# A two-layer decoder trunk on one core: split weights two tiles further ahead, gate weights in the activation ring, rotary tables after the first stage

## The chip, the core and the metric

The kernel runs on one core of a Trainium2 chip. The metric is device time in microseconds from start to end of one execution, as the median of several runs. TensorE (PE) multiplies matrices, VectorE (DVE) and ScalarE (ACT) work element by element, GpSimd (POOL) does a few steps, SyncE (SP) issues nearly all DMAs.

## The reference

Two layers, 256 positions, width 2048, all in 32-bit floats. In each layer one normalised input goes through one projection (`w_in`) into five parts: queries, keys and values of eight heads of differential attention, and the two branches of a gated linear recurrence (RG-LRU). Both groups are concatenated, go through `w_out` and are added to x. Then comes an MLP with a causal convolution of three taps.

```python
h = rmsnorm(x, attn_norm[l])
q, k, v, xb, gb = jnp.split(h @ w_in[l], splits, axis=-1)
q, k = apply_rope(q, cos, sin), apply_rope(k, cos, sin)
attn_out = diff_attention(q, k, v, lam, subln[l], lam_init)
lru_out = rglru_branch(xb, gb, ...)     # conv of 4 taps, two gates, scan, norm
x = x + concat(attn_out, lru_out) @ w_out[l]
h = rmsnorm(x, mlp_norm[l])
x = x + conv_glu_mlp(h, w_up[l], ffn_conv_w[l], ffn_conv_b[l], w_down[l])
```

`cos` and `sin` come from the positions. The gates are eight blocks of 128 x 128 weights each, for two gates. `decay` below is a softplus of `lru_lambda` by a series, and `lambda` the scalar of the differential attention.

## The kernel before, in words

**Weights.** All weights stream through the core once, 1 MB at a time: `raw` tiles of 128 x 2048 floats, 200 units per layer, in the order of the list `stream`. There are three raw buffers. Each `raw` is cut into two tiles of 128 x 1024. ACT rounds a tile to the matmul's format (`hi`, line 174), DVE subtracts to get the remainder (`lo`, line 181). Activations are split in the same way (`xh`: high and low side by side, lines 296 and 300). A product is then two matmuls: `hi` times both activation parts (512 columns) and `lo` times the high part (256 columns). Such a pair for one 128 x 128 piece of weights is called a block; a tile is eight blocks.

**Order.** The order of every engine is the order in which the Python code emits instructions; there is no scheduler. `run` (line 246) emits 16 blocks at a time, two tiles: first one side of all 16, then the other; the next run starts with the side on which this one ended, so every second run starts with its low parts. While it takes blocks, `next_blocks` emits the `hi` tile that lies `HI_LEAD` ahead at a tile's start, and in its middle the `lo` tile that lies `LO_LEAD` ahead and the DMA that a finished raw tile makes room for. All other work is deferred: `defer(n, fn)` emits `fn` once TensorE's instructions have come n blocks further. A list of such steps (`steps`) is the schedule of each piece: tables of cosine and sine (`setup_tables`), `setup_decay`, `setup_lambda`, the LRU (`lru_front`, `lru_back`), a head (`attention`). Since an engine takes its instructions in order, a step that waits holds up what was emitted behind it.

**Stages of a layer.** First the eight column pairs of the LRU (`rb`, 32 blocks each) and the value projection (`pv`, in quarters of 16 blocks); then the heads (`qk`), the output projection (`po`) and the MLP (`pu`, `pd`), each with all 24 tiles of a half's hidden values in the ring `actp`, which has 24 buffers. Layer 0 begins with `first_stage`: inputs arrive feature by feature, and for each pair of features k, k+1 TensorE does two LRU column pairs (`recurrent`) and half of the values (`values`). `prepare` makes high and low parts there in halves of 512 columns (lines 888 and 889), and TensorE's instructions are emitted `LEAD` features behind. Gate weights lie in a fixed tile `gw_sb` of 1 MB, loaded by `later_inputs` in layer 0 and at the start of layer 1. After two column pairs, `lru_back` does their gates (`gp`, line 535), four ACT functions for each, square root, scan and `gate`, then a square (line 588) and a sum for the norm. For a head: `turns`, `rope`, `scores`, softmax, `difference` (line 695), `turn` (transposes on TensorE, line 703), `values`, a norm and `back`.

Lines after the change are some ten to twenty higher than before from line 536 on.

## Time and profile before

| | us |
|---|---|
| median of three runs | 2334.37 |
| lowest, highest | 2333.59, 2338.35 |
| the profiled execution | 2339.55 |
| its span, first to last instruction | 2337.7 |
| TensorE busy in the span | 2302.3 (98%) |
| VectorE busy | 1655.5 (71%) |
| ScalarE busy | 1290.1 (55%) |
| mean granted TensorE clock | 0.995 |

The busy time of TensorE is that of its matmul records, whose ends are modelled; neighbouring matmuls overlap in it. In a row of a timeline stand start, length, engine, line, operation, tiles written and read, shape and count; in brackets the idle time of the engine ahead of it and what ended that. A row of waits names who waited, for whom, the total in us, how often and the longest. A row of windows gives a stretch, its length, the busy time of each engine with its instructions, the granted clock (1.00 is full speed), the share of the DMA engines and GB/s.

### The profile page before, as it was taken

Reading aid. Unit: us, or ns where it says so; the run is one execution under the profiler, and the core shown is the slowest. Engines: PE = TensorE matmul, PEld = TensorE weight load, DVE = VectorE, ACT = ScalarE, POOL = GpSimd, SP = SyncE. Lnnn points to the kernel's source line nnn. Section 1 sums busy time; section 2 is a strip of 40 time slices with the busy share of each in tenths; the row PEclk is TensorE's granted clock in tenths of the full one; section 3 lists DMA queues with packets and bytes.
Section 4 is the critical chain, followed back from the end, with each engine's and each line's share of the span. In section 5 each row is a group of like instructions: output and inputs, shape, how many; then the busy total and the mean of one; then the engine's idle time right before and its main releaser. Section 6 shows DMA issues by size and latency. Waiting matters only on the chain.

```text
span 2337.7 us, 33496 instructions
## 1 busy us (share of the span) xinstructions
PE 2302.3 (98%) x13196; PEld 2020.9 (86%) x13196; DVE 1655.5 (71%) x2321; ACT 1290.1 (55%) x1930; POOL 38.5 (2%) x148
## 2 busy tenths in 40 slices
PE   8999999999999999999999999999999999999998
PEld 6887888888888888888888888888888888888887
DVE  7677877777754677775567797777776557777654
ACT  6775645555543455554457666455555335555543
POOL 0000000000000000000000000000000000000000
PEclk9999999999999999999999999999999999999999
DMA  7344445455555455555455444555454545455543
GB/s 266 145 162 155 155 165 196 181 196 195 186 180 199 181 197 191 188 182 200 177 198 180 180 152 160 183 193 196 181 194 185 198 181 198 180 197 193 187 180 126
DMA packets 63229, 428.93 MB, mean 183 GB/s; under 512 B 7136, under 2 KB 7904, under 8 KB 12640
## 3 DMA queue, kind: packets, MB, share of 16 engines
q1 hardware_dynamic: 62352, 425.74, 49.7%
q8 instruction: 103, 1.69, 0.3%
q10 hardware_dynamic: 720, 1.07, 0.1%
q14 instruction: 54, 0.44, 0.1%
HBM read 424.68 MB, written 2.10 MB: 183 GB/s over the span
## 4 chain that ended last, share of the span: by engine, by line
PE 70%; issue 12%; DVE 11%; ACT 6%; DMA 1%; SPq 0%; POOL 0%; DVEq 0%; POOLq 0%; ACTq 0%
PE pu L264 34%; PE pd L264 17%; PE qk L264 5%; PE po L264 4%; DVE lo L181 4%; PE rb L264 3%; PE po_None L264 2%; ACT hi L174 2%; DVE cc L779 1%; DMA raw<-in_w 1%; DVE us L765 1%; PE pv L845 1%; PE pv L846 1%; PE pv L844 1%; DVE us L276 0%
## 5 line engine op out<-in xcount | busy, mean ns | idle before, releaser
L181 DVE TENSOR_TENSOR lo<-raw,hi 128x1024 fp32r<-128x1024 f32 x784 | 938.5, 1219 | 194.1 <-ACT hi L174 110.4
L174 ACT ACTIVATE hi<-raw 128x1024 fp32r<-128x1024 f32 x784 | 806.9, 1052 | 343.1 <-PE pd L264 183.2
L264 PE MATMUL pu<-xhm,hi 128*128 128x512 f32 x3008 | 700.9, 390 | 0.6 <-DVE x L959 0.4
L264 PEld LDWEIGHTS pu<-xhm,hi 128*128 128x128 f32 x3008 | 558.4, 188 | 113.4 <-issue 0.8
L264 PEld LDWEIGHTS pu<-xhm,lo 128*128 128x128 f32 x3008 | 373.7, 192 | 9.5 <-DVE lo L181 1.1
L264 PE MATMUL pu<-xhm,lo 128*128 128x256 f32 x3008 | 377.0, 283 | 1.6 <-DVE lo L181 0.9
L264 PE MATMUL pd<-h,hi 128*128 128x512 f32 x1512 | 352.0, 390 | 0.0
L264 PEld LDWEIGHTS pd<-h,hi 128*128 128x128 f32 x1512 | 280.7, 188 | 56.3
L779 DVE SCALAR_TENSOR_TENSOR cc<-us,cst_sb,cc 128x256 f32<-128x256 f32 x384 | 177.8, 483 | 42.0 <-ACT cc L772 35.2
L264 PEld LDWEIGHTS pd<-h,lo 128*128 128x128 f32 x1512 | 187.9, 192 | 3.7
L264 PE MATMUL pd<-h,lo 128*128 128x256 f32 x1512 | 189.2, 283 | 0.0
L772 ACT ACTIVATE cc<-us,cst_sb 128x256 f32<-128x256 f32 x192 | 105.6, 595 | 98.4 <-DVE us L765 98.4
L276 DVE TENSOR_TENSOR us<-pu,us 128x512 f32<-128x512 f32 x92 | 63.3, 688 | 122.9 <-ACT us L273 122.9
L963 DVE TENSOR_TENSOR x<-pd,x 128x512 f32<-128x512 f32 x56 | 38.7, 691 | 128.6 <-PE pd L264 127.7
L273 ACT ACTIVATE us<-pu 128x512 f32<-128x512 f32 x92 | 55.2, 600 | 114.8 <-PE pu L264 114.8
L785 ACT ACTIVATE cc<-cc 128x256 f32<-128x256 f32 x96 | 40.2, 419 | 66.8 <-DVE cc L779 66.3
L791 ACT ACTIVATE h<-cc 128x256 fp32r<-128x256 f32 x96 | 40.1, 417 | 53.0 <-DVE cc L788 50.0
L765 DVE TENSOR_TENSOR us<-us,row_m 128x512 f32<-128x512 f32 x96 | 65.4, 682 | 3.2
L264 PE MATMUL qk<-xhn,hi 128*128 128x512 f32 x256 | 62.0, 394 | 0.0
L264 PE MATMUL qk<-xhs,hi 128*128 128x512 f32 x256 | 61.9, 393 | 0.0
L264 PE MATMUL rb<-xhn,hi 128*128 128x512 f32 x256 | 61.0, 393 | 0.0
L264 PEld LDWEIGHTS qk<-xhn,hi 128*128 128x128 f32 x256 | 46.9, 188 | 11.6 <-issue 2.3
(257 smaller groups left out, 2123.7 us busy)
## 6 DMA issues: line engine op xcount, KB each, us to landing
raw<-in_w SPq DMA_DIRECT2D x392, 1024.0 KB, 4.8
raw<-in_w SPq DMA_DIRECT2D x12, 512.0 KB, 8.2
raw<-in_w SPq DMA_DIRECT2D x8, 256.0 KB, 6.4
gw_sb<-in_gw SPq DMA_DIRECT2D x2, 1024.0 KB, 10.0
x<-in_x SPq DMA_DIRECT2D x7, 256.0 KB, 7.8
out<-x ACTq DMA_DIRECT2D x4, 256.0 KB, 2.4
out<-x SPq DMA_DIRECT2D x4, 256.0 KB, 2.4
cst_sb<-in_cst SPq DMA_DIRECT2D x1, 425.0 KB, 10.6
```

The costliest lines, as they stand in the source:

```text
L174: act.activation(out=hi_t[v], in_=raw_part(v), func=AF.Copy)
L181: dve.tensor_tensor(out=lo_t[v], in0=raw_part(v), in1=hi_t[v].bitcast(F32), op=ALU.subtract)
L264: pe.matmul(out=dst, lhsT=taken[i][side], rhs=o, start=first and side == sides[0], stop=last and side == sides[1], skip_group_check=True,)
L273: act.activation(out=dst, in_=pb[:, :, SEQ:], func=AF.Copy)
L276: dve.tensor_tensor(out=dst, in0=pb[:, :, 0:SEQ], in1=dst, op=ALU.add)
L765: dve.tensor_tensor(out=dst, in0=dst if source is None else source, in1=row, op=ALU.mult)
L772: act.activation(out=cc[:, s], in_=us[:, s, 1:SEQ + 1], func=AF.Identity, scale=ccol(l, C_FCW + 3 * tiles[s]), bias=ccol(l, C_FCB + tiles[s]),
L779: dve.scalar_tensor_tensor(out=cc[:, s], in0=us[:, s, j + 1:j + 1 + SEQ], scalar=ccol(l, C_FCW + 3 * tiles[s] + j), in1=cc[:, s], op0=ALU. ...
L785: act.activation(out=cc[:, 0], in_=cc[:, 0], func=AF.Gelu_apprx_tanh)
L791: act.activation(out=t[:, 0], in_=cc[:, 0], func=AF.Copy)
L844: pe.matmul(out=pv[:, tb], lhsT=th_, rhs=wh, start=(k == 0), stop=False)
L963: dve.tensor_tensor(out=x_sb[i], in0=pb[:, :, s * SEQ:(s + 1) * SEQ], in1=x_sb[i], op=ALU.add)
```

## The change

The edits:

- High and low parts: `HI_LEAD` from 3 to 5, `LO_LEAD` from 2 to 4, two more buffers for each. The feature lead of the first stage goes from 2 to 4.
- `pos_sb` moves to the ring `t1`; the fixed tile `gw_sb` is gone. `load_gates` loads the gate weights in four DMAs into four buffers of the ring `actp`, in each layer, and the last gates give them back.
- In layer 0 the first value quarter of the second half (unit 20) comes between the column pairs 2 and 3 instead of behind all of them.
- The tables start 150 blocks into the kernel instead of 48, and their steps lie further apart; decay starts at 60 instead of 40, lambda at 100 instead of 150, the late DMAs at 24 instead of 16.
- LRU: square three blocks later, its sum four.
- Heads 0 to 6: `scores` to `turned` three blocks later, `values` to `low` four. Head 7 keeps its steps, but for `values` to `normed`, which come one block later.
- First stage: from the third unit on, parts are made as in the rest of the kernel, 1024 columns at a time; the norm's sum starts 24 blocks after the last pair instead of 13.
- The end of the first stage makes parts up to five tiles ahead of the first tile behind it.

```diff
-LEAD = 2
+LEAD = 4
-HI_LEAD = 3
-LO_LEAD = 2
+HI_LEAD = 5
+LO_LEAD = 4
-HI_BUFS = 5
-LO_BUFS = 4
+HI_BUFS = 7
+LO_BUFS = 6
...
-    pos_sb = t1.tile([P, SEQ], I32, tag="ti1", name="pos_sb", bufs=1)
-    gw_sb = const.tile([P, 2 * LT, P], F32, name="gw_sb")
+    pos_sb = t1.tile([P, SEQ], I32, tag="t1", name="pos_sb")
...
-            order = [*range(4, 16)]
+            order = [4, 5, 20, *range(6, 16), 21, 22, 23]
...
-            (0, angle), (6, coarse), (14, less_coarse), (18, turns), (32, reduced), (40, lambda: mirrored(1)),
-            (46, lambda: folded(1)), (50, lambda: mirrored(-1)), (56, lambda: folded(-1)), (60, sines), (70, signed),
+            (0, angle), (8, coarse), (24, less_coarse), (30, turns), (50, reduced), (64, lambda: mirrored(1)),
+            (76, lambda: folded(1)), (84, lambda: mirrored(-1)), (96, lambda: folded(-1)), (104, sines), (120, signed),
...
-                        out=tl["gp"][i][:, g * SEQ:(g + 1) * SEQ], lhsT=gw_sb[:, g * LT + j0 + i], rhs=xc[:, i],
+                        out=tl["gp"][i][:, g * SEQ:(g + 1) * SEQ], lhsT=gate_w[g * LT + j0 + i], rhs=xc[:, i],
...
+            if j0 == LT - 2:
+                gate_w.clear()
...
-            (n + 37, square), (n + 42, summed),
+            (n + 40, square), (n + 46, summed),
...
-            n = 83 if h == HEADS - 1 else 94
+            if h == HEADS - 1:
+                a, b, c = 19, 51, 83
+            else:
+                a, b, c = 22, 54, 98
...
-                (5, turns), (8, rope), (19, scores), (22, maxima), (29, exps), (35, weights), (38, second),
-                (41, difference), (51, turn), (54, turned), (62, values), (65, squares), (69, mean), (74, normed),
-                (n, back), (n + 3, high), (n + 7, low),
+                (5, turns), (8, rope), (a, scores), (a + 3, maxima), (a + 10, exps), (a + 16, weights),
+                (a + 19, second), (a + 22, difference), (b, turn), (b + 3, turned), (b + 12, values), (b + 15, squares),
+                (b + 19, mean), (b + 24, normed), (c, back), (c + 3, high), (c + 7, low),
...
-        state["hi"] = state["lo"] = tiles
+        state["hi"] = state["lo"] = 4 * FINE // 2
...
+            if u >= FINE:
+                if k % 2:
+                    hi_to(2 * u + 1)
+                    lo_to(2 * u + 1)
+                return
...
-                    n.finish(13)
+                    n.finish(24)
...
-                if i >= KD - 4:
-                    t = tiles + (i - KD + 4) // 2
-                    hi_to(t + 1)
-                    lo_to(t)
+                if i >= KD - 6:
+                    hi_to(tiles + (i - KD + 6) + 1)
+                    lo_to(tiles + (i - KD + 6))
...
+    def load_gates(l):
+        for i in range(4):
+            t = actp.tile([P, 4, P], F32, tag="a", name=f"gw{l}_{i}")
+            sync.dma_start(out=t, in_=gw[l][:, 4 * i:4 * i + 4])
+            for b in range(4):
+                gate_w[4 * i + b] = t[:, b]
...
-                defer(16, later_inputs)
-                defer(40, setup_decay)
-                defer(48, setup_tables)
-                defer(150, setup_lambda)
+                defer(24, later_inputs)
+                defer(60, setup_decay)
+                defer(100, setup_lambda)
+                defer(150, setup_tables)
...
+                if l == 0 and j == 2:
+                    pv = value_banks(l, 1)
+                    value_quarter(l, 1, 0, pv)
+            if l:
+                pv = value_banks(l, 1)
-            for quarter in range(4):
+            for quarter in range(1 - l, 4):
```

How the instructions move is seen at three places. The first is DVE's queue around the last unit of the first stage before the change: `rest` and `turns` are the tables, `xhs` the activations' low parts, `lo` the weights'.

```order
L318 TENSOR_TENSOR acc_n_first<-acc_n_first,xq_n_first_513 128x512
L397 SCALAR_TENSOR_TENSOR rest<-turns,ang 128x2x256
L399 SCALAR_TENSOR_TENSOR rest<-turns,rest 128x2x256 x2
L399 SCALAR_TENSOR_TENSOR rest<-many,rest 128x2x256
L409 TENSOR_TENSOR rest<-rest,turns 128x2x256
L300 SCALAR_TENSOR_TENSOR xhs_553<-x_107,gain_sb,xhs_553 128x256
L889 TENSOR_TENSOR lo_557<-raw_386,hi_556 128x512
L889 TENSOR_TENSOR lo_561<-raw_386,hi_560 128x512
L300 SCALAR_TENSOR_TENSOR xhs_564<-x_107,gain_sb,xhs_564 128x256
L889 TENSOR_TENSOR lo_557<-raw_386,hi_556 128x512
L889 TENSOR_TENSOR lo_561<-raw_386,hi_560 128x512
```

After the change the same queue, one unit earlier, holds only that unit's own steps between the end of the decay's series (`q`) and its close.

```order
L447 SCALAR_TENSOR_TENSOR q<-q,z_415 128x16 x8
L300 SCALAR_TENSOR_TENSOR xhs_485<-x_106,gain_sb,xhs_485 128x256
L300 SCALAR_TENSOR_TENSOR xhs_488<-x_106,gain_sb,xhs_488 128x256
L181 TENSOR_TENSOR lo_495<-raw_341,hi_491 128x1024
L181 TENSOR_TENSOR lo_497<-raw_341,hi_493 128x1024
L318 TENSOR_TENSOR acc_n_first<-acc_n_first,xq_n_first_499 128x512
L452 SCALAR_TENSOR_TENSOR q<-q,z 128x16
```

The tables have left this stage, and four low parts of 512 columns have become two of 1024.

The second place is SP's queue, before the change, where the late inputs are loaded; `raw_323` is the seventh weight unit (raw6).

```order
L160 DMA raw_266<-in_w 128x1024 x2
L950 DMA gw_sb<-in_gw 128x2048
L951 DMA kc_sb<-in_kc 128x130
L952 DMA pos_sb<-in_pos 128x256
L953 DMA cst_sb<-in_cst 128x850
L954 DMA lam_sb<-in_lamv 128x512
L160 DMA raw_323<-in_w 128x1024 x2
```

After the change (`raw_281` is the seventh unit here, `raw_341` the eighth, raw7):

```order
L160 DMA raw_281<-in_w 128x1024 x2
L963 DMA gw_0_300<-in_gw 128x512
L963 DMA gw_1_302<-in_gw 128x512
L963 DMA gw_2_304<-in_gw 128x512
L963 DMA gw_3_306<-in_gw 128x512
L969 DMA kc_sb<-in_kc 128x130
L970 DMA pos_sb<-in_pos 128x256
L971 DMA cst_sb<-in_cst 128x850
L972 DMA lam_sb<-in_lamv 128x512
L160 DMA raw_341<-in_w 128x1024 x2
```

The late inputs stand one weight unit later, and are eight issues instead of five.

The third place is ACT's queue in layer 0's LRU stage, at the back steps of the column pairs 2 and 3 (`sq_2` is their root, `gl` a gelu, the last row the square), before:

```order
L567 ACTIVATE sq_2_1044<-th_2_664 128x2x256
L510 ACTIVATE xc_4_910<-xg_4_911,cst_sb 128x256
L511 ACT_TABLE_LOAD
L511 ACTIVATE gl_4_907<-xg_4_911 128x256
L174 ACTIVATE hi_1083<-raw_939 128x1024
L570 ACTIVATE th_2_664<-u_2_1011,mones 128x512
L174 ACTIVATE hi_1096<-raw_986 128x1024
L588 ACTIVATE gl_2_663<-bx_2_665 128x512
```

and after:

```order
L569 ACTIVATE sq_2_1068<-th_2_644 128x2x256
L510 ACTIVATE xc_4_933<-xg_4_934,cst_sb 128x256
L511 ACT_TABLE_LOAD
L511 ACTIVATE gl_4_930<-xg_4_934 128x256
L412 ACT_TABLE_LOAD
L412 ACTIVATE trig_sb<-rest 128x512
L174 ACTIVATE hi_1109<-raw_961 128x1024
L572 ACTIVATE th_2_644<-u_2_1035,mones 128x512
L174 ACTIVATE hi_1122<-raw_1009 128x1024
L174 ACTIVATE hi_1165<-raw_1009 128x1024
L590 ACTIVATE gl_2_643<-bx_2_645 128x512
```

The sine of the tables (`trig_sb`) and a load of its function stand between the gelu and the next high part, and one more high part stands ahead of the square.

More of the change, by code (lines that the diff above doesn't have):

```diff
@@ L140, in trunk_kernel @@
                 order += [16 + quarter, 8 + 2 * quarter, 9 + 2 * quarter]
-        order += [*range(20, U_IN)]
+            order += [20, 21, 22, 23]
+        order += [*range(24, U_IN)]
         for half, i in PROJECTED:
@@ L916, in first_stage @@
                 prepare(k + 1)
-                raw_t.pop(k // 2)
+                raw_t.pop(k // 2, None)
                 square_pair(k // 2, n)
@@ L941, in first_stage @@
                     lo_t.pop(i + g)
-                if i >= KD - 4:
-                    t = tiles + (i - KD + 4) // 2
-                    hi_to(t + 1)
-                    lo_to(t)
+                if i >= KD - 6:
+                    hi_to(tiles + (i - KD + 6) + 1)
+                    lo_to(tiles + (i - KD + 6))
         state["at"] = tiles * SB
         defer(4, lambda: values_out(0, 0, pv))
+    gate_w = {}
+    def load_gates(l):
[4 more added lines that the diff above has]
+                gate_w[4 * i + b] = t[:, b]
     def later_inputs():
-        sync.dma_start(out=gw_sb, in_=gw[0])
+        load_gates(0)
         sync.dma_start(out=kc_sb[:, P:], in_=kc[:, P:])
@@ L1046, in trunk_kernel @@
             if l:
-                sync.dma_start(out=gw_sb, in_=gw[l])
+                load_gates(l)
             else:
-                defer(16, later_inputs)
-                defer(40, setup_decay)
-                defer(48, setup_tables)
-                defer(150, setup_lambda)
+                defer(24, later_inputs)
+                defer(60, setup_decay)
+                defer(100, setup_lambda)
+                defer(150, setup_tables)
                 first_stage()
@@ L1061, in trunk_kernel @@
                     value_quarter(l, 0, j - 3, pv)
-            pv = value_banks(l, 1)
-            for quarter in range(4):
+                if l == 0 and j == 2:
[4 more added lines that the diff above has]
+            for quarter in range(1 - l, 4):
                 value_quarter(l, 1, quarter, pv)
```

## The prediction

> **What bounds the kernel now.** I read the page first, then the stages by windows, then TensorE's waits by stage, and last the engines' timelines around the longest waits.
>
> ```profile
> span 2337.7 us, 33496 instructions
> PE 2302.3 (98%) x13196; PEld 2020.9 (86%) x13196; DVE 1655.5 (71%) x2321; ACT 1290.1 (55%) x1930; POOL 38.5 (2%) x148
> ```
>
> TensorE (PE) is busy for 98% of the span. So the change can win only what TensorE now waits, and what it loses to a lower clock. The windows show where (after the times: PE, PEld, DVE, ACT, POOL busy, granted clock, DMA share, GB/s):
>
> ```profile
> 5.00:56.00 51.00, 43.41 (x208) 34.74 (x207) 40.69 (x83) 30.55 (x59) 5.49 (x9) 1.00 0.78 278
> 56.00:63.00 7.00, 6.53 (x18) 5.37 (x19) 4.46 (x9) 3.72 (x5) 0.82 (x3) 0.51 0.52 164
> 97.00:104.00 7.00, 6.18 (x19) 5.26 (x20) 5.54 (x7) 2.53 (x4) 0.10 (x1) 0.51 0.59 215
> 104.00:128.00 24.00, 21.68 (x125) 19.06 (x124) 16.37 (x23) 19.64 (x29) 0.10 (x1) 1.00 0.30 113
> 128.00:131.40 3.40, 3.40 (x11) 2.81 (x11) 3.36 (x5) 0.93 (x1) 0.00 (x0) 0.53 0.85 308
> 160.00:291.00 131.00, 126.14 (x740) 106.36 (x739) 105.12 (x180) 82.84 (x188) 5.75 (x7) 1.00 0.42 157
> 400.00:1180.00 780.00, 780.00 (x4528) 692.31 (x4528) 536.42 (x714) 404.20 (x537) 4.43 (x43) 1.00 0.52 190
> ```
>
> From 400 to 1180 us (the MLP) TensorE never stops: more lookahead is worth nothing there. Layer 0 up to 291 us holds the waits and three spells at about half clock. A spell loses half of what TensorE worked in it: 6.53 x 0.49 = 3.2 us, 6.18 x 0.49 = 3.0 and 3.40 x 0.47 = 1.6, together 7.8.
>
> The waits of TensorE by stage (total, times, longest), in the order 0 to 60, 60 to 160, 160 to 300, 360 to 400 and 1180 to 1540 us:
>
> ```profile
> PE rb L904 <- DVE lo L889: 3.4, 3, 1.7
> PE rb L899 <- DVE xhs L300: 2.0, 2, 1.6
> PE ss_n_first L327 <- DVE acc_n_first L322: 1.5, 1, 1.5
> ...
> PE rb L264 <- DVE lo L181: 5.0, 3, 2.3
> PE pv L845 <- DVE lo L181: 0.5, 1, 0.5
> ...
> PE at L703 <- DVE pr L695: 3.9, 5, 1.3
> PE qk L264 <- DVE lo L181: 0.6, 1, 0.6
> ...
> PE pu L264 <- DVE lo L181: 0.9, 1, 0.9
> ...
> PE rb L264 <- DVE lo L181: 2.7, 3, 1.8
> ```
>
> These are 6.9 us in the first stage, 5.5 in layer 0's LRU stage, 4.5 in its attention, 0.9 at the start of its MLP and 2.7 in layer 1's LRU stage: 20.5 us. With the clock 28.3 us, which is all there is to win. Nearly every wait is for a low part or for another step of VectorE (DVE).
>
> **Part by part.** *First stage.* Two pieces of the DVE's and ACT's timelines show why low parts come late (lo of two halves; counters and angle of the tables; the decay's series):
>
> ```profile
> 31.51 1.29 DVE L889 TENSOR_TENSOR lo<-raw,hi 128x512 fp32r<-128x512 f32 x2
> 34.20 1.94 DVE L447 SCALAR_TENSOR_TENSOR q<-q,z 128x16 f32<-128x16 f32 x8
> 36.85 0.88 DVE L383 SCALAR_TENSOR_TENSOR ang<-many,ang 128x256 f32<-128x256 f32 x2
> 38.04 1.69 DVE L889 TENSOR_TENSOR lo<-raw,hi 128x512 fp32r<-128x512 f32 x2
> ...
> 47.13 1.42 DVE L399 SCALAR_TENSOR_TENSOR rest<-turns,rest 128x512 f32<-128x512 f32 x2
> 50.58 0.69 DVE L409 TENSOR_TENSOR rest<-rest,turns 128x512 f32<-128x512 f32 x1 [1.30 <-POOL turns L405]
> ...
> 37.88 1.30 POOL L390 TENSOR_SCALAR turns<-ang 128x256 f32<-128x256 f32 x2 [2.60 <-DVE ang L383]
> 45.87 1.28 ACT L412 ACT_TABLE_LOAD   x1
> 56.12 0.63 ACT L412 ACTIVATE trig_sb<-rest 128x512 f32<-128x512 f32 x1 [8.97 <-DVE rest L409]
> ```
>
> DVE is busy 40.69 of 51 us. The tables' rows here (0.88, 1.42, 0.69 and 1.30 of waiting) stand directly ahead of low parts that TensorE waits for. With them gone, halves merged into 1024-wide steps, and two more buffers, the late ones (all but about 1.4 us, early waits for data) should disappear: 6.9 - 1.4 = 5.5 us. The decay stays, but TensorE now has up to three units in hand instead of two. What is late next is data: 8 MB of weights, x, and the constants. Constants move behind raw6 and ahead of raw7; SP issues in order, so raw7 waits for its turn behind eight issues. A unit lasts TensorE 16 blocks. I cost that at nothing, because raw7 is needed two units later; uncovered it is the second rival below. Without the waits at 52 to 56 us I expect the spell at 56 us gone too: 3.2 us.
>
> *LRU stage of layer 0.* A block (one 512-wide high and one 256-wide low matmul) costs 11.11 / 32 = 0.347 us by this piece of the chain:
>
> ```profile
> 342.88 11.11 PE po L264 x64
> ```
>
> A run makes the low parts of the run behind it, and in a run that starts on low parts they are due 11 to 13 blocks after being issued: 3.8 to 4.6 us. Two more tiles add one run, 16 blocks or 5.5 us. The three waits (5.0 us, longest 2.3) are shorter than that, so as waits for lo they go, with the 0.5: 5.5 us, and with them the two spells, 3.0 + 1.6. But another wait stands right behind. ACT and DVE run a loop from one pair's gate matmuls to the taps of the next pair (rows of PE, then of ACT, then of DVE):
>
> ```profile
> 74.50 1.89 PE L535 MATMUL gp<-xc,gw_sb 128*128 128x256 f32 x8
> 97.82 2.08 PE L264 MATMUL rb<-xhs,lo 128*128 128x256 f32 x8 [1.24 <-DVE lo L181]
> 127.22 1.60 PE L264 MATMUL rb<-xhs,lo 128*128 128x256 f32 x8 [2.32 <-DVE lo L181]
> ...
> 104.14 0.47 ACT L545 ACTIVATE th<-gp,hb_sb 128x256 f32<-128x256 f32 x1 [4.62 <-PE gp L535]
> 122.52 0.63 ACT L588 ACTIVATE gl<-bx 128x512 f32<-128x512 f32 x1 [3.46 <-DVE bx L584]
> 123.06 1.04 ACT L174 ACTIVATE hi<-raw 128x1024 fp32r<-128x1024 f32 x1
> ...
> 127.08 1.52 DVE L515 SCALAR_TENSOR_TENSOR xc<-xg,cst_sb,xc 128x256 f32<-128x256 f32 x3
> ```
>
> From 104.14 to 127.08 + 1.52 it takes 24.5 us. TensorE needs 64 blocks (22.2 us) and eight gate matmuls (1.89): 24.1 us. So gate matmuls would wait about 0.4 us per pair in place of lo. The square behind `gate`, three blocks later, falls behind one more high part, and ACT's wait of 3.46 shrinks by its 1.04: loop 23.5. The value quarter between pairs gives the first loop 16 blocks (5.5 us) more, enough for the table's DVE rows there. The sine, however, falls between two gelus of the second loop: a load, the sine and a load back, 1.28 + 0.63 + 1.28 = 3.2 us, so 26.7 against 24.1. I charge 2.6 us, and 1.6 for a spell like the one at 128 us, which followed the wait of 2.32. Net gain: 10.1 - 4.2 = 5.9 us; the ends are 10.1 (the sine is hidden by parts made ahead) and 0 (every loop waits as now).
>
> POOL's table steps move along. In the rows above two low parts took 1.69 us while POOL worked, 1.29 without: 0.4 per pair of steps, about 1.6 us over the tables, which the first loop's 5.5 us hide. [...]
>
> *Attention.* Scores to `difference` and `turn` move three blocks back, 1.04 us. Of five waits for `pr` (3.9, longest 1.3) about 1.0 would remain, and the 0.6 for lo goes. But DVE has 105.12 of 131 us to do already, and one value quarter fewer now lies between LRU and heads, so the last pair's force and scans fall into head 0. I take 3.2 of 4.5; the ends are 0 and 4.5.
>
> *The rest.* The wait of 0.9 for lo at the MLP's start goes. Layer 1's three (2.7) go as lo, less 0.5 for one wait for the loop: 2.2. Gate weights in the activation ring wait for the last `pd` to release four hidden tiles; on SP only raw205 queues behind them, which is not due for four tiles, so nothing. Layer 1's first gates come 25 blocks after its second pair of columns. MLP: nothing.
>
> **Sum.** 5.5 + 3.2 + 5.9 + 3.2 + 0.9 + 2.2 = 20.9 us. The profiled execution took 2339.55 us (its span is 2337.7), 5.2 above the median of 2334.37; 20.9 off gives 2318.7 for a profiled one and 2313.5 for the median.
>
> **Rivals.**
>
> (a) *Slower: the loop bounds layer 0.* If ACT and DVE, not lookahead, set the pace, the tables go onto the loop's path: 3.2 us on ACT, on DVE 5.1 (0.88, four `rest` steps at 0.71, two folds at 0.69), 1.6 for POOL: 9.9. Each of three gate waits then passes the 2.32 us that had a spell behind it and costs a long spell's 3.2, 9.6 for the 4.6 now. That is +14.9, less 8.7 won in the first stage: +6.2, 2341. It decides once waits for gp in layer 0 add up to more than 14 us. For it speaks ACT's 19.64 of 24 us; against it, that ACT's rows above show 4.62 and 3.46 of idling. 0.05.
>
> (b) *The first stage is bound by data.* DMA is at 0.78 over it. If raw7 comes late behind the constants, the 8.7 us there stay: 2322. 0.12.
>
> (c) *The spells don't hang on these waits.* No single wait ahead of them lasted over 2.32 us, so something else may lower the clock at these places. Then the spells stay as they are, and 3.2 + 3.0 (those at 56 and 97 us; the third is charged already) come off the sum: 2320. Against it: the spells of 97 and 128 us begin within 1 us of the waits at 97.82 and 127.22, and in the 780 us without a wait the clock is 1.00. 0.08. [...]
>
> (d) *Nothing takes the place of the waits:* all 28.3 us go, 2306. 0.20.
>
> (e) *The lookahead is not reached,* because three raw buffers stay: high parts five tiles ahead wait for DMA. Then of the sum only the first stage's 5.5 us are left: 2329. Against it: from 400 to 1180 us DMA is at 0.52. 0.06.
>
> The forecast itself: 0.49.
>
> The range takes in the ends of the terms: 2304 (all of 28.3, and 2 for what a wait's row leaves out) to 2326 (first stage alone, 8.7). About 0.2%, 4.7 us, is what a measurement of this kernel can tell from no change. Case (e) lies so near that bound that I count 0.04 of it as same; (a) is slower, the rest faster: 0.91, 0.04, 0.05.
>
> **What would show it.** Right: no waits for lo L181 at rb in either layer; the clock at 1.00 around 56 us; waits for gp on xc of 2 to 3 us in one loop, where the sine stands on ACT; the MLP unchanged. Wrong: waits for raw or for xhs before 56 us (b); half-clock spells without waits (c); waits for xc at every pair (a); idle ACT ahead of hi with DMA as releaser (e).

## The result and the profile after

| | median of its runs, us | lowest to highest | ratio to before, 95% interval |
|---|---|---|---|
| before (4 runs) | 2335.91 | 2333.59 to 2338.35 | |
| after (4 runs) | 2319.94 | 2317.67 to 2321.37 | 0.9931 [0.9913, 0.9948] |
| after, again (5 runs, before 2335.65) | 2317.61 | 2316.85 to 2321.92 | 0.9929 [0.9916, 0.9941] |

The change makes the kernel 16 to 18 us faster, within the range, where 20.9 was forecast. The profiled execution of after took 2321.12 us.

```profile
span 2319.3 us, 33304 instructions
PE 2292.8 (99%) x13196; PEld 2016.9 (87%) x13196; DVE 1654.7 (71%) x2309; ACT 1290.5 (56%) x1919; POOL 40.9 (2%) x148
```

TensorE does the same 13196 matmuls, and the span is 18.4 us shorter than the 2337.7 of before. The starts of the first matmul of each stage in PE's timeline give the stages; "again" is a second profiled execution of after, and "best" is the last experiment:

| stage, us | before | after | again | best | after less before | forecast |
|---|---|---|---|---|---|---|
| first stage | 59.08 | 53.94 | 50.54 | 46.68 | -5.1 | -8.7 |
| rest of the LRU, layer 0 | 106.46 | 100.90 | 100.92 | 97.97 | -5.6 | -5.9 |
| heads, layer 0 | 112.11 | 107.84 | 107.82 | 103.71 | -4.3 | -3.2 |
| output projection | 93.99 | 94.13 | 94.15 | 94.14 | +0.1 | 0 |
| MLP | 803.27 | 803.26 | 803.26 | 803.25 | 0.0 | -0.9 |
| LRU, layer 1 | 143.89 | 140.47 | 140.47 | 140.45 | -3.4 | -2.2 |
| heads, layer 1 | 105.16 | 103.45 | 103.45 | 103.43 | -1.7 | 0 |
| output projection and MLP, layer 1 | 908.60 | 909.98 | 909.99 | 910.00 | +1.4 | 0 |

The rows of the heads and of what follows them have to be read together. Eight small matmuls of the heads run in the output projection after the change, in both layers (heads 632 matmuls where before had 640, output projection 552 where it had 544), because the last steps of the heads come four blocks later. With the heads' steps put back (an experiment below) layer 1's heads take 104.66 us and its output projection 93.26; in after they take 103.45 and 94.14. So 0.9 us of the gain in a layer's heads is work that has moved.

The windows of after, cut like those of before (the times of PE, PEld, DVE, ACT, POOL, the granted clock, DMA share, GB/s):

```profile
5.00:49.00 44.00, 40.35 (x197) 32.71 (x196) 34.01 (x63) 30.20 (x48) 0.00 (x0) 1.00 0.96 330
49.00:56.00 7.00, 6.01 (x20) 5.31 (x21) 3.87 (x13) 2.10 (x3) 0.74 (x2) 0.51 0.60 238
97.00:128.00 31.00, 27.28 (x151) 23.38 (x150) 27.99 (x39) 26.94 (x38) 3.07 (x7) 1.00 0.45 162
195.80:199.20 3.40, 3.40 (x10) 2.67 (x9) 3.33 (x6) 0.00 (x0) 0.00 (x0) 0.50 0.63 222
```

There were three stretches at half clock, and there are two: one at the end of the first stage again, seven us earlier, and a new one in the first head. Between them the clock is full. DMA is now busy for 0.96 of the first 44 us. PE's waits, whole span:

```profile
PE gp L535 <- DVE xc L515: 4.6, 3, 2.9
PE ss_n_first L327 <- DVE acc_n_first L322: 3.1, 1, 3.1
PE at L705 <- DVE pr L697: 2.1, 1, 2.1
...
PE pu L264 <- ACT xhm L296: 1.4, 1, 1.4
```

No row of a wait for the low parts of L181 is left, in any stage. In their place stand four waits behind other work: the first sum of squares (`ss_n_first`, 1.5 before and 3.1 now), the gate matmuls (`gp`), the first head's turn (`at`) and the start of the MLP.

**The first sum.** DVE's rows ahead of the fold for which PE waits, at the end of the first stage of after:

```profile
46.33 0.68 DVE L318 TENSOR_TENSOR acc_n_first<-acc_n_first,xq_n_first 128x512 f32<-128x512 f32 x1
...
47.60 1.22 DVE L181 TENSOR_TENSOR lo<-raw,hi 128x1024 fp32r<-128x1024 f32 x1
48.73 0.42 DVE L466 TENSOR_TENSOR pr<-lam_sb 128x256 f32<-128x256 f32 x1
49.19 0.42 DVE L467 TENSOR_REDUCE s<-pr 128x4 f32<-128x256 f32 x1
49.52 0.41 DVE L322 TENSOR_TENSOR acc_n_first<-acc_n_first 128x256 f32<-128x256 f32 x1
```

The last squares are added from 46.33 to 47.01. The fold could follow, and comes at 49.52: the end of the decay, a low part for a later stage and lambda's two rows (block 100, where before had block 150) stand ahead of it, 2.5 us of the 3.1.

**The gates.** DVE's rows ahead of the second pair's taps (L515), for which the wait of 2.9 us stands:

```profile
93.38 0.69 DVE L397 SCALAR_TENSOR_TENSOR rest<-turns,ang 128x512 f32<-128x512 f32 x1
94.10 1.42 DVE L399 SCALAR_TENSOR_TENSOR rest<-turns,rest 128x512 f32<-128x512 f32 x2
95.55 0.69 DVE L399 SCALAR_TENSOR_TENSOR rest<-many,rest 128x512 f32<-128x512 f32 x1
...
97.30 0.68 DVE L276 TENSOR_TENSOR xg<-rb,xg 128x512 f32<-128x512 f32 x1
98.02 0.87 DVE L507 TENSOR_TENSOR xg<-xg,row_n_first 128x512 f32<-128x512 f32 x1
...
99.94 1.51 DVE L515 SCALAR_TENSOR_TENSOR xc<-xg,cst_sb,xc 128x256 f32<-128x256 f32 x3
```

Four table rows, 2.8 us, stand ahead of evacuation, scaling and taps. This is the loop that contains the value quarter, and not the loop of the sine.

### The profile page after: what moved, and what is told of

It is laid out like the page before. It is cut to its first block, busy times and chain, and to the rows that moved or that the text cites. A ratio compares the mean times of both kernels' runs of the same rounds, so it can differ in the third digit from the quotient of the medians.

```text
span 2319.3 us, 33304 instructions
## 1 busy us (share of the span) xinstructions
PE 2292.8 (99%) x13196; PEld 2016.9 (87%) x13196; DVE 1654.7 (71%) x2309; ACT 1290.5 (56%) x1919; POOL 40.9 (2%) x148
## 4 chain that ended last, share of the span: by engine, by line
PE 83%; issue 9%; DVE 4%; ACT 2%; DMA 1%; SPq 0%; POOLq 0%; DVEq 0%; ACTq 0%; POOL 0%
PE pu L264 42%; PE pd L264 17%; PE qk L264 7%; PE po L264 5%; PE rb L264 4%; PE po_None L264 2%; DVE lo L181 1%; PE pv L849 1%; PE pv L850 1%; PE pv L851 1%; DMA x<-in_x 1%; PE s L655 1%; DMA raw<-in_w 1%; ACT hi L174 0%; PE gp L535 0%
## 5 line engine op out<-in xcount | busy, mean ns | idle before, releaser
L181 DVE TENSOR_TENSOR lo<-raw,hi 128x1024 fp32r<-128x1024 f32 x796 | 954.0, 1220 | 191.7 <-ACT hi L174 110.8
L174 ACT ACTIVATE hi<-raw 128x1024 fp32r<-128x1024 f32 x796 | 818.0, 1051 | 356.3 <-PE pd L264 189.4
L264 PEld LDWEIGHTS qk<-xhs,hi 128*128 128x128 f32 x256 | 48.3, 193 | 11.8 <-issue 2.3
```

The lines of the kernel that those rows point to most:

```text
L174: act.activation(out=hi_t[v], in_=raw_part(v), func=AF.Copy)
L181: dve.tensor_tensor(out=lo_t[v], in0=raw_part(v), in1=hi_t[v].bitcast(F32), op=ALU.subtract)
L264: pe.matmul(out=dst, lhsT=taken[i][side], rhs=o, start=first and side == sides[0], stop=last and side == sides[1], skip_group_check=True,)
```

## The experiments

There are three sets of kernels; those of one set ran on one chip, beside the kernel before. The first has the lookahead undone and the three kernels around the fold. The second has the second execution of after, the lookahead alone, the reductions moved behind the taps and the heads' steps put back. The third has the rest; the first execution of after belongs to none of them. The median of before was 2334.69, 2335.65 and 2335.89 us in them, so comparisons with after across sets have about 1 us of doubt beside the scatter of the runs. Ratios are to before, with 95% intervals.

### The lookahead undone, and the lookahead alone

```diff
-HI_LEAD = 5
-LO_LEAD = 4
+HI_LEAD = 3
+LO_LEAD = 2
```

> The changed kernel with high parts made three and low parts two tiles ahead again (buffers, gate ring, tables and first stage stay as changed). Theory (the lookahead ended the waits for low parts): the waits of the LRU loops, of the first projection and of layer 1's first loops come back, 5.5 + 0.9 + 2.7 us of them in the profile of before, and half-speed stretches with them: 7 to 11 us more than the changed kernel, about 2329 us, with rows 'PE rb <- DVE lo' in the waits. Rival (those waits went because the tables and the constants moved, not because of the lookahead): within 2 us of the changed kernel, no row of a wait for lo at rb.

```profile
PE rb L264 <- DVE lo L181: 7.8, 7, 3.1
...
PE qk L264 <- DVE lo L181: 1.7, 1, 1.7
...
PE pu L264 <- DVE lo L181: 0.9, 1, 0.9
```

2324.2 us (2322.84 to 2332.09), 0.9959 [0.9945, 0.9972]. The waits for low parts are back, and no wait for `gp` is left. The rest of layer 0's LRU takes 106.10 us (after 100.90) and layer 1's 142.96 (140.47): the lookahead is worth 5.2 + 2.5 us there. The total is 4 to 7 us above after, where 7 to 11 were expected: in its profile the first stage took 48.78 us, 2 to 5 less than in after's two (it varies from run to run, as the next kernels show), and the first head had neither after's wait of 2.1 us nor the stretch behind it (heads 106.23 us, after 107.84).

The other way round, the lookahead was put into the kernel before, with its two more buffers for each, the gate ring and the place of `pos_sb` in the ring `t1` that make room for them, and nothing else:

```diff
-HI_LEAD = 3
-LO_LEAD = 2
+HI_LEAD = 5
+LO_LEAD = 4
...
-        sync.dma_start(out=gw_sb, in_=gw[0])
+        load_gates(0)
```

> The kernel before with the lookahead alone: high parts five and low parts four tiles ahead, the gate weights in the activation ring to make room; tables, first stage and attention as before. Theory (the lookahead ends the waits for low parts; the waits at the gates in the changed kernel come from the tables that now stand in the loops): no row of a wait for the low parts of L181 at rb, at most 1 us of waits at the gates in all, and 9 to 14 us less than before, about 2323 us. Rival (low parts made earlier stand ahead of the taps on DVE whatever the tables do): waits at the gates of 2 to 3 us, and 5 us or less gained, 2330 us.

```profile
PE at L705 <- DVE pr L697: 4.2, 4, 2.1
PE gp L534 <- DVE xc L514: 3.9, 3, 3.1
```

2329.76 us (2326.53 to 2331.57), 0.9973 [0.9963, 0.9984]: 5.9 us of the 16 to 18. The rival's time and waits came out. The waits at the gates come although the tables are in the first stage here: the loop of ACT and DVE stands right behind the low parts, and the lookahead uncovers it. The rival's mechanism has a part in it: DVE's rows run without a gap from 83.90 us to the second pair's taps at 95.26, and two of them are low parts (1.22 us each, at 91.66 and 94.12) that stand between the `gate` step of the pair before and the taps. How much of the 3.1 us is theirs was not tested. The heads' waits (4.2 against 3.9 us before) don't go by lookahead either.

The two kernels fit together: all the edits without the lookahead gain 10.5 us on before (2334.69 to 2324.2), the lookahead alone 5.9, together 16.4 of the 16 to 18. But the profile here is of the fastest run: its LRU stages gain more than the median does (100.14 us against 106.46, 140.70 against 143.89), and its first stage, whose own steps are those of before, takes 54.21 us against 59.08. A single profile does not tell what an edit in the first stage is worth.

### What stands ahead of the fold

One kernel puts lambda back to block 150, one puts the sum ten blocks later, and one sends the last weight unit of the first stage (raw7) ahead of gate weights, positions and lambda vectors:

```diff
-                defer(100, setup_lambda)
+                defer(150, setup_lambda)
```

> The changed kernel with the lambda dot products put back from block 100 to block 150. Theory (DVE's queue ahead of the fold sets the 3.1 us wait of the first sum of squares): the product and the reduction (48.73 to 49.52) no longer stand ahead of the fold, so the wait is 0.8 us shorter, 2.3 us; the half-speed stretch may stay, as a wait of 2.1 us in the first attention head had one: 0.8 us less, about 2319 us; 4 us less if the stretch goes with it. Rival (the fold waits for the last unit's data, not for the queue): no difference in the wait, 0 us, or up to 1 us more, since the products now stand in the first gate loop.

```diff
-                    n.finish(24)
+                    n.finish(34)
```

> The changed kernel with the end of the first norm put ten blocks later (24 to 34), so that PE has ten more blocks of matmuls to do before the sum of squares. Theory (the wait for the sum brings on the half-speed stretch behind it): the wait of 3.1 us goes, and the stretch of 6.8 us at half speed with it, 3.1 + 3.4 = 6.5 us less, about 2313.5 us. Rival (the stretch does not come from this wait): 3.1 us less, about 2317 us, with a stretch still between 45 and 60 us. Second rival (PE then waits for the last unit's low parts or for the norm's row instead): 0 to 2 us less.

```diff
     def later_inputs():
-        load_gates(0)
-        sync.dma_start(out=kc_sb[:, P:], in_=kc[:, P:])
-        sync.dma_start(out=pos_sb, in_=pos[0].partition_broadcast(P))
         sync.dma_start(out=cst_sb[:, DEPTH * C_LRU:], in_=cst[:, DEPTH * C_LRU:])
+
+    def last_inputs():
+        load_gates(0)
+        sync.dma_start(out=kc_sb[:, P:], in_=kc[:, P:])
+        sync.dma_start(out=pos_sb, in_=pos[0].partition_broadcast(P))
...
+                defer(40, last_inputs)
```

> The changed kernel with the gate weights, the identity's remainder, the positions and the lambda vectors sent after the last unit of the first stage instead of ahead of it (the constants of the layers stay ahead). Theory (the last unit lands late because eight transfers stand ahead of it, and everything of DVE up to the fold is late by that): its second half lands 3 to 6 us earlier than 42.65 us, the wait of 3.1 us before the sum goes, and the half-speed stretch with it: 3 to 6.5 us less, about 2315 us. Rival (DVE's own queue of decay, low parts and lambda is what is late, not the data): the data land earlier and the wait stays over 2 us: 0 to 1 us less.

| | us | ratio | wait of the first sum | first stage of its profile |
|---|---|---|---|---|
| lambda at 150 | 2314.65 (2313.17 to 2315.75) | 0.9913 [0.9900, 0.9926] | none | 46.78 |
| sum ten blocks later | 2315.52 (2314.37 to 2318.47) | 0.9919 [0.9907, 0.9930] | 1.1 | 48.47 |
| raw7 first | 2319.47 (2314.10 to 2323.17) | 0.9931 [0.9917, 0.9945] | 1.0 | 47.94 |

By their medians the two edits that touch only the order of the steps win 2 to 5 us on after. For lambda that is clear: its five runs lie below all nine of after (2316.85 to 2321.92). Of the five with the sum later one lies among them, and its interval overlaps after's. No half-speed stretch stands at the end of the first stage in any of the three profiles. Lambda's two rows are only 0.8 us, yet the wait went altogether in that profile: the data came earlier in it as well. ACT's rows for the second half of the last unit, in the second execution of after:

```profile
41.24 1.06 ACT L174 ACTIVATE hi<-raw 128x1024 fp32r<-128x1024 f32 x1 [2.96 <-DMA raw<-in_w]
42.87 1.06 ACT L174 ACTIVATE hi<-raw 128x1024 fp32r<-128x1024 f32 x1 [0.57 <-DMA raw<-in_w]
```

and with raw7 first, where nothing waits for DMA:

```profile
36.84 1.99 ACT L174 ACTIVATE hi<-raw 128x1024 fp32r<-128x1024 f32 x2
```

With lambda at 150 these rows start at 38.42 and 39.68, some 3 us ahead of after's. Nearly 2 us of that stand there before the edited step: the weight DMAs that SP starts at 18.16 and 17.91 us in after's two profiles start at 16.12. Nor does a short wait need an edit here: with the heads' steps put back, where the first stage is that of after, these rows start at 39.52 and 40.92 and the sum waits 0.8 us. So a single profile's wait of 0 to 1.1 us proves little; what lambda's edit is worth rests on its runs, and how its gain divides between queue and data is not shown. With raw7 first ACT takes its data 4 to 5 us earlier, nearly 2 of them again from an early start (16.22 us), and the wait is 1.0, but the median is no better than after's. Its profile is of a run of 2315.56; what its runs above 2320 met is not in it, and stays open.

### The clock's windows

After ran once more, unchanged:

> The changed kernel once more, beside the three variants of this set. Theory (TensorE's clock is granted anew every 3.41 us, and goes to half for the next such window where PE was busy for about 1.5 us or less of one; a wait of 2 to 3 us therefore brings on a half-speed stretch or not by where it falls in the windows): the waits are those of its first profile within 0.3 us, about 3.1 us before the sum of squares, 2.9 and twice about 1 us at the gates, 2.1 us in the first head, but the stretches may stand behind others of them; its runs scatter over 4 to 6 us. In every profile windows with 1.51 us of PE or less are followed by half speed, those with 1.60 us or more are not. Rival (each stretch belongs to its wait): half speed again from about 49 for 6.8 us and from about 196 for 3.4 us, none behind the 2.9 us wait.

The waits were the same to within 0.6 us, not the 0.3 expected (2.6 for the sum, 2.9 at the gates, 2.1 in the first head), and only one stretch at half clock was left, in the first head. The borders of all stretches of an execution lie on one grid of 3.41 us. Windows of that grid in the first execution of after (length, PE busy, clock, DMA share, GB/s):

```profile
45.62:49.04 3.42, 1.23 (x6) 1.00 0.62 194
96.82:100.24 3.42, 1.77 (x8) 1.00 0.25 103
192.40:195.81 3.41, 1.51 (x11) 1.00 0.57 178
195.81:199.22 3.41, 3.41 (x10) 0.50 0.63 221
```

in the second execution:

```profile
45.08:48.50 3.42, 1.50 (x7) 1.00 0.70 259
96.28:99.70 3.42, 1.77 (x8) 1.00 0.59 192
188.44:191.86 3.42, 1.28 (x10) 1.00 0.45 141
191.86:195.27 3.41, 3.41 (x12) 0.50 0.63 207
```

and in the kernel with the sum ten blocks later, whose wait at the gates is as long as after's, 2.9 us:

```profile
92.60:96.01 3.41, 0.85 (x4) 1.00 0.14 19
96.01:99.43 3.42, 3.06 (x7) 0.50 0.73 295
```

The wait of 2.9 us leaves 1.77 us of PE in its window in after and has no stretch behind it; there it leaves 0.85, and the next window runs at half clock. Taking the windows of all fourteen profiles from 20 to 400 us that began at full clock: 15 had 1.43 us of PE or less, and each was followed by half clock; none with 1.73 or more was. Between 1.49 and 1.70 five were and two were not (the 1.50 of this second execution is one of the two), so the 1.51 against 1.60 of the expectation was too sharp. The expected scatter is there (2316.85 to 2321.92): three of its five runs lie below 2318, two above 2321.

A kernel with matmuls of no use in the three places tests the same from the other side; the idea is that filling a window keeps the clock:

```diff
+    def filler(bank, n):
+        for _ in range(n):
+            pe.matmul(
+                out=bank, lhsT=xh[0][:, 0, 0:P], rhs=xh[0].rearrange("p a b -> p (a b)"), start=True, stop=True,
+                skip_group_check=True,
+            )
...
+            if self.name == "n_first":
+                filler(ps, 9)
...
+            if l == 0 and j0 == 2:
+                filler(tl["gp"][0], 9)
...
+            if l == 0 and h == 0:
+                filler(tb, 7)
```

> The changed kernel with matmuls of no use put in PE's queue where it waits: nine of 512 columns ahead of the first sum of squares, nine ahead of the second gate pair, seven ahead of the first head's turn (2.0, 2.0 and 1.6 us of PE), each into the bank that the next matmul overwrites. It adds work and takes no wait's cause away. Theory (half speed follows where a 3.41 us window has little PE work in it): no stretch at half speed from 10 to 2300 us, so the time is that of the changed kernel less its stretches, 2316 us or 1.7 us below, in runs that lie within 3 us of one another. Rival (a stretch belongs to what PE waits for, or comes by itself): stretches at 49, 97 or 191 us as in the two profiles of the changed kernel, and a time equal to its or up to 2 us above.

```profile
48.37:51.79 3.42, 1.49 (x9) 1.00 0.70 287
51.79:55.20 3.41, 3.41 (x14) 0.50 0.64 231
```

2316.41 us (2315.66 to 2319.14), 0.9916 [0.9902, 0.9930]. The stretch in the first head is gone, though PE still has to wait there (0.5 us). Its window, 191.73 to 195.14 us, has 2.88 us of PE, some 1.5 of them the filler's; I estimate that about 1.3 would have been left without it, as little as was followed by half clock each time (15 windows with 1.43 us or less). But this is one profile, and the kernel with the sum ten blocks later had no stretch there either with its full wait of 2.1 us, which fell across two windows of 2.3 and 2.4 us of work. At the sum PE stood for 1.9 us beyond the filler, the window had 1.49 us of work, and a stretch followed. So "no stretch at all" was wrong for its profile, and the theory of the window held. 1.2 us below the better median of after is too little to call a gain by itself.

### Gates and heads

```diff
-            (0, angle), (8, coarse), (24, less_coarse), (30, turns), (50, reduced), (64, lambda: mirrored(1)),
-            (76, lambda: folded(1)), (84, lambda: mirrored(-1)), (96, lambda: folded(-1)), (104, sines), (120, signed),
+            (0, angle), (8, coarse), (24, less_coarse), (30, turns), (72, reduced), (78, lambda: mirrored(1)),
+            (84, lambda: folded(1)), (89, lambda: mirrored(-1)), (98, lambda: folded(-1)), (104, sines), (120, signed),
```

> The changed kernel with the four steps that reduce the angles moved on DVE from ahead of the evacuation, the scaling and the taps of the second gate pair to behind its taps (block 50 to 72 of the tables), the folds a little later, sine and sign where they were. Theory (2.8 us of these four steps ahead of the taps set the 2.9 us wait at the second pair's gates): that wait falls under 1 us and no other grows by more than 0.5 us: 2 us less than the changed kernel, 3.7 us where a half-speed stretch stood behind it. Rival (ACT's queue sets that wait, as the first tap stands behind the tanhs and exponentials of the pair before): the wait stays over 2.5 us and the time the same.

```profile
PE gp L535 <- DVE xc L515: 2.3, 2, 1.4
```

2314.86 us (2312.46 to 2316.27), 0.9910 [0.9897, 0.9924], 2.8 us below after in the same set, and all its runs below all of after's. The wait of 2.9 us is gone; the next loop's grew from 0.8 to 1.4, a little more than the 0.5 expected; the LRU stage falls from 100.9 to 98.59 us. The place of four rows in DVE's queue was the cause.

```diff
-                defer(100, setup_lambda)
-                defer(150, setup_tables)
+                defer(64, setup_tables)
+                defer(100, setup_lambda)
```

> The changed kernel with the tables made in the first stage again (at block 64, with the step distances of before). Theory (the tables only change places: what their steps cost as waits in the first stage, they cost at the gates in the loops): the wait at the second gate pair falls from 2.9 us under 1 us, a wait for low parts or for the sum of squares in the first stage grows by 2 to 4 us, and the time is within 2 us of the changed kernel. Rival (leaving the first stage is what won its 5 us): 4 us or more above the changed kernel, with rows of waits for lo and xhs of 4 us together.

```profile
PE ss_n_first L327 <- DVE acc_n_first L322: 8.1, 1, 8.1
...
PE gp L535 <- DVE xc L515: 0.2, 1, 0.2
```

Besides the lines shown, the steps of the tables have their old distances. 2319.59 us, 0.9929 [0.9917, 0.9942], within 2 us of after, as the theory had it; but the wait of the sum is 8.1 us, far more than the 2 to 4 of the expectation. The first stage takes 57.77 us and the LRU stage 96.00: what the tables cost in the one place, they cost in the other.

```diff
-            order = [4, 5, 20, *range(6, 16), 21, 22, 23]
+            order = [*range(4, 16), 20, 21, 22, 23]
...
-                if l == 0 and j == 2:
-                    pv = value_banks(l, 1)
-                    value_quarter(l, 1, 0, pv)
-            if l:
-                pv = value_banks(l, 1)
-            for quarter in range(1 - l, 4):
+            pv = value_banks(l, 1)
+            for quarter in range(4):
```

> The changed kernel with the first quarter of the second half of the values made after the gate loops again, in place of inside the first one (the tables are started 16 blocks earlier, so that their reductions keep their place ahead of the second pair's evacuation). Theory (the eight blocks, 2.8 us of PE work, are slack for ACT and DVE in that loop): the wait at the second pair's gates grows from 2.9 to 5 us or more, a half-speed stretch stands behind it every time, and the time is 2.5 to 4.5 us above the changed kernel. Rival (the loops' chain does not lead over the eight blocks): within 1 us of it.

```profile
PE gp L535 <- DVE xc L515: 4.8, 2, 4.6
```

2321.08 us (2319.09 to 2322.04), 0.9932 [0.9919, 0.9946]; the wait at the second pair grows to 4.6 us and has a stretch of 6.8 us behind it, and the LRU stage takes 103.27 us. (A quarter is 16 blocks, not the eight of the expectation.) So the quarter's room does help, by 1.7 us of wait. By the medians the kernel is 1.1 to 3.5 us above after, partly under the theory's 2.5 to 4.5; its runs overlap with after's, so the time by itself is unclear. In the first head the wait is 0.5 us here, where after has 2.1.

```diff
-                a, b, c = 22, 54, 98
+                a, b, c = 19, 51, 94
```

> The changed kernel with the scores, the turn and the way back of the heads at the blocks of before (19, 51, 94 in place of 22, 54, 98). Theory (the three blocks more, 1.04 us, are what ended the waits for the difference in the heads behind the first): waits at the turn of up to 1.0 us come back in two or three heads and the one of 2.1 us grows to about 3 us: 2 to 4 us more than the changed kernel. Rival (the lookahead ended them, as DVE no longer stood with low parts ahead of the difference): 0 us, only the first head's wait 1 us longer.

2318.17 us, 0.9926 [0.9913, 0.9940], no difference from after in time. But the waits changed places: two of together 1.3 us came back in later heads, and the 2.1 us of the first head went. ACT's rows show why. In after:

```profile
183.49 0.91 ACT L296 ACTIVATE ml<-bx,cst_sb 128x256 fp32r<-128x256 f32 x2 [3.66 <-DVE bx L612]
...
185.36 1.28 ACT L678 ACT_TABLE_LOAD   x1
186.66 0.37 ACT L678 ACTIVATE pr<-s,mx 128x128 f32<-128x128 f32 x1
```

with the heads' steps back:

```profile
175.61 1.28 ACT L678 ACT_TABLE_LOAD   x1
176.91 0.37 ACT L678 ACTIVATE pr<-s,mx 128x128 f32<-128x128 f32 x1
...
178.51 0.91 ACT L296 ACTIVATE ml<-bx,cst_sb 128x256 fp32r<-128x256 f32 x2
```

Three blocks later the first head's exponentials (L678) come behind the LRU's last parts `ml`, for which ACT waits 3.66 us on DVE; three blocks earlier they go ahead of it. In this kernel the edit helps the later heads and makes the first head's wait; the expectation had that wait growing to 3 us. It is not the only cause, as the lookahead alone has a wait of 2.1 us there with the heads' old steps, and the quarter behind the loops leaves 0.5 with the new ones.

### The four mended

```diff
-            (0, angle), (8, coarse), (24, less_coarse), (30, turns), (50, reduced), (64, lambda: mirrored(1)),
+            (0, angle), (8, coarse), (24, less_coarse), (30, turns), (72, reduced), (78, lambda: mirrored(1)),
...
+            elif h == 0 and l == 0:
+                a, b, c = 19, 54, 98
...
-                    n.finish(24)
+                    n.finish(30)
...
-                defer(100, setup_lambda)
+                defer(150, setup_lambda)
```

> The changed kernel with four edits: the lambda dot products at block 150, the end of the first norm six blocks later (24 to 30), the four reductions of the tables behind the taps (block 72), and the first head's scores at block 19 with its turn left at 54. Theory (the waits of the changed kernel are DVE and ACT queue orders that can be mended one by one, and without a wait over 1.8 us no half-speed stretch comes): against the span of 2315.8 us of the second profile of the changed kernel the sum's wait loses 2.3, the second gate pair's 2.4, the first head's 1.6, the stretch 1.7 us: a span of 2307.8, a time of about 2309.6 us, no stretch at half speed between 10 and 2300 us, and runs within 3 us. Rival (the waits move on, to the third and fourth gate pair or into the first gate loop where the dots now stand): 2312 to 2314 us, with a wait over 1.8 us at the gates.

Its waits (those left out stand at the start and the end of the kernel or are under 1 us), then its first three stages:

```profile
PE gp L535 <- DVE xc L515: 1.8, 2, 0.9
...
PE pu L264 <- ACT xhm L296: 1.4, 1, 1.4
```

```profile
5.70:52.40 46.70, 46.35 (x232) 39.23 (x233) 39.28 (x70) 34.84 (x53) 0.74 (x2) 1.00 0.96 344
52.40:150.40 98.00, 96.16 (x516) 83.07 (x515) 84.00 (x120) 83.35 (x118) 10.14 (x14) 1.00 0.50 180
150.40:254.10 103.70, 103.70 (x634) 89.30 (x633) 91.38 (x157) 68.11 (x156) 5.68 (x6) 1.00 0.45 157
```

2307.65 us (2306.99 to 2310.14), 0.9878 [0.9865, 0.9892]: 28 us faster than before and 10 to 12 faster than after, 2 better than the theory. No wait in the layers is over 1.4 us, no stretch at half clock is left from 7 to 2297 us, and PE is busy for 46.35 of the first stage's 46.70 us. Two of the four edits, the sum six blocks later and the first head's early scores, were not run by themselves.

## Why the prediction was right, and where its steps failed

The sum of 20.9 is set against 18.4 us between the profiled executions. The median moved by 16 to 18, as the profiled execution of before lay 3.6 us above its median of four and that of after 1.2. The medians of 2317.6 and 2319.9 lie between the 2313.5 of the forecast and the 2320 of rival (c), so the time alone does not choose between them; the profiles do. Part of the agreement is luck, as the terms show.

- **First stage, 5.5 us, and the stretch behind it, 3.2: 5.1 in one execution, 8.5 in the other.** The waits for lo and xhs (5.4) went altogether. The step that failed is the other wait of the 6.9, that for the first sum: its 1.5 us were counted among those that go, and with them the stretch ("Without the waits at 52 to 56 us I expect the spell at 56 us gone too"). PE came sooner to the sum, its wait grew to 2.6 and 3.1, and a stretch followed in one profile of two. Ahead of the fold stand steps charged at nothing: the late data of raw7, a low part, and lambda's rows at block 100, whose return gains 3 to 5 us by the median; the low part was not tried by itself. Rival (b) was half right: the data came late, but the 8.7 us did not stay.
- **LRU stage of layer 0, net 5.9: 5.6.** The size was right by luck and the place wrong. I charged 2.6 for the sine's loop and 1.6 for a stretch, 4.2 together; the waits came to 4.6, and no stretch followed in after's two profiles. Behind the same wait of 2.9 us a stretch of 3.4 us stands in the profiles with raw7 first, with the sum later and with the heads' steps back, by the place of the windows: 1.28, 0.85 and 1.21 us of PE are left in the window ahead of it, where after's two profiles have 1.77. The sine's loop waits 0.8 us. The first loop waits 2.9, although I let its quarter hide the tables' DVE rows: these stand ahead of the taps, and the 5.5 us of the quarter take only 1.7 off the wait. That the loop of ACT and DVE stands right behind the low parts was right, as the lookahead alone shows.
- **Heads, 3.2: 4.3 in layer 0, of which 0.9 is moved work.** The waits of the later heads went, and with the quarter or the heads' blocks put back some return (2.1 and 1.3 us in all heads). The first head's wait, expected at about 1.0, was 2.1 with a stretch of 1.7 us behind it. The waits in the rows thus fell only from 4.5 us to 2.1 and the stretch: 0.7 us. What the rest of the gain is, no row of waits shows, so that the size agrees is in part luck. The reason given, that DVE would be late in head 0 with one quarter fewer ahead of it, was half right: PE waits behind ACT's queue, ACT there waits 3.66 us for DVE, and with the quarter put back the wait is 0.5.
- **The MLP's start, 0.9: nothing.** ACT's row of the part that PE waits for there, before and after:

```profile
379.70 0.51 ACT L296 ACTIVATE xhm<-x,cst_sb 128x256 fp32r<-128x256 f32 x1 [1.53 <-DVE x L959]
```

```profile
365.01 0.51 ACT L296 ACTIVATE xhm<-x,cst_sb 128x256 fp32r<-128x256 f32 x1 [1.53 <-DVE x L977]
```

  It starts 2.9 us behind the MLP's first matmul in both (376.82 and 362.12), waiting for x. In before 0.9 us of that time went on the low part and 0.2 on this part of x; with the low part ready PE waits 1.4 us for x alone. I took one releaser for the only one.
- **Layer 1, 2.2: 3.4 in the LRU,** without the wait for the loop that I had kept back. Its heads gain 1.7 and the output projection and the MLP behind give 1.4 back; PE has no wait in these heads in either profile, and 0.9 us is the moved work; heads and what follows together gain 0.3.
- **The rivals.** (a) fell: the waits at the gates are 4.6 us, not 14. (e) fell: with the lookahead undone the waits for low parts come back. (d) did not happen in after: four other waits took the place of the old ones; with the three longest mended the kernel comes to 2307.65, near (d)'s 2306. (c) in its form fell: stretches come and go with waits. But the prediction's other reading, a stretch for each such wait, fell too: of the windows counted above, none with 1.73 us of PE or more was followed by half clock.

The step of the windows' grid is 3.41 us, and its place differs from run to run: a border lies at 49.04 us in the first execution of after and at 48.50 in the second. A window followed by half clock was not empty here: that of before from 52.72 to 56.14 us had 1.37 us of work, and each with 1.43 or less was followed by it.

## What to carry to other kernels

When a wait is removed, look up what PE meets next in its own queue, and what stands ahead of that in the queue of the engine that makes it; here three waits of 2 to 3 us each had a few such rows ahead of them that could go elsewhere, and moving them won 10 to 12 us. Room in a loop (blocks of PE work) does less than it measures: 5.5 us of it took 1.7 off a wait, moving four rows from ahead of the awaited one took off all 2.9. Where single waits of 2 to 3 us remain, compare medians and several profiles, since half clock behind them comes or not by the windows' place: behind the wait of 2.9 us it came where the window had 0.85 us of work left, and not where it had 1.77.

## What was not expected of the hardware

- In these profiles the clock changes only at the borders of windows of 3.41 us, and a half-speed window that is itself not filled is mostly followed by another: in after 49.04 to 52.45 us had 2.46 us of PE and the next was at half speed too. Of nine such windows in the fourteen profiles from 20 to 400 us, with up to 3.08 us of PE, eight were followed by half speed, and one with 3.06 (the sum ten blocks later, 96.01 to 99.43 us) was not; every half-speed window that PE filled (3.41 us in after from 195.81 us) was followed by full speed. So by its place in the grid a stop of 2 to 3 us costs its own length alone, or with it half of what PE works at half speed: 1.7 us for one filled window, 3.2 for the stretch at 56 us of before.
- Matmuls of no use in the place of a wait probably kept the clock up in the first head, where after had lost 1.7 us in both of its profiles: 2.88 us of PE in the window, where after had 1.51 and 1.28. The evidence is one profile.
